# Branch B of a hybrid decoder layer: log-decays in one full-row product, the samples' state products in row quarters, outputs one step later, and a gated residual added out of PSUM

## The chip, the cores and the metric

The kernel runs on 1 core of one Trainium2 chip. The metric is the device time of one execution in microseconds (us), lower is better; a kernel's number is the median of its runs.

## The reference

One inference step of one decoder layer (D = 1024) in float32, for a prompt of 512 tokens and for 8 sample sequences of 8 new tokens each with their own state. The 576 token columns share all weights. The layer is

- `x += 1/2 gate1 * SwiGLU1(mod(rmsnorm(x)))`
- `x += gate2 * W_out(sum_i sigmoid(gate_i(h)) * proj_i(branch_i(h)))` with the branches A (dilated window attention), B (Mamba-2 SSD scan) and C (a gated linear recurrence)
- `x += 1/2 gate3 * SwiGLU2(mod(rmsnorm(x)))`, then a last rmsnorm

The gates come per sequence: one vector for the prompt, one for each of the 8 samples. Branch B matters here. Per head (16 heads of 64 channels, state size 128, 2 groups) and with `acum` the running sum of the log-decays inside a chunk of 128 tokens, the scan computes

```
y_diag[l]   = sum_{s<=l} (C_l . B_s) exp(acum_l - acum_s) xdt[s]
state_out   = sum_s B_s  xdt[s] exp(acum_end - acum_s)
h_next      = exp(acum_end) h + state_out
y[l]        = y_diag[l] + exp(acum_l) C_l . h
```

The prompt is 4 chunks (c = 0 to 3) from a zero state. The samples are 8 chunks of 8 tokens, each from its given `state_ssm`; each writes a new state (1024 x 128).

## The kernel before

**The main work.** `run` goes through a list of units: each is a block of 128 output channels with a weight `raw` of 128 x 1024. ACT casts it to fp32r (`wh`, L278), DVE or, in some units, POOL subtracts to get the remainder `wl` (L280), and TensorE makes for each of 8 k-chunks three fp32r products of 128 x 288 in two halves (L342: H with `wh`, H with `wl`, L with `wh`) into a two-bank PSUM tile `mm`. Six matmuls are one k-chunk, and the main products follow one another on TensorE all along the kernel.

**Lanes.** Between k-chunks `step` advances generators ("lanes") that issue the layer's other work: attention, norms, the recurrence, and `ssd` for branch B. A unit lists its lanes with a number of steps (5 for `ssd`), so the order of every engine is fixed by these numbers at build time; `later` puts a cast or a subtraction one or two turns back. Small products take one of four PSUM banks of the pool `px` in turn; a new tile waits until the bank's last reader is done.

**Branch B, prompt** (`ssd`, L1031). For 20 items (c, hg), c = 0 to 4 and hg = 0 to 3 (four heads each; c = 4 is the 64 sample columns), the work is a pipeline of stages, one item further with each step of the lane: `stage_a` (n), `stage_b` (n-1), `stage_c` (n-2), `stage_d` (n-3).

- `diagonal(c)` (L1083) lays the 16 heads' log-decays out as 16 rows x 4L columns and splits them into a high part `dgH` (ACT) and a remainder `dgL` (DVE).
- `stage_a` broadcasts four heads' decays to 128 partitions: two fp32r matmuls from 16 rows, `dgH` then `dgL`, 512 columns each (256 for c = 4), into `pb` (L1103). So there are 16 pairs of 512 columns and 4 of 256. ACT makes exponents `M` and `Cs` from `pb`.
- `stage_c` multiplies: `M` with the masked C.B on DVE (L1128), `Cs` with C on POOL (L1131).
- `stage_d` makes the outputs `py` on TensorE (L1143, L1146), and DVE adds them into `acc` (L1150).
- `prelude(c+1)` transposes the next chunk in the same steps (`px_tok`, `px_cb`, two `px_xt`, L1047 to L1071). At hg = 0 `state(c-1)` makes the new state: DVE decays it (L1158), two products `pst` (L1162), and DVE adds them in two halves (L1167).

**Branch B, samples** (L1204 to L1258). For each of 8 samples: load the state `st` (`ld`, two ahead), transpose it (`px_st`, 8 transpositions, ACT copies to `sT`), then in `products` 16 small output products `yo` (L1221) and, in two halves q, four products `px_ns` (L1228) of 64 rows, where a mask `bm` leaves one sample's 8 tokens. DVE decays and adds the state (L1231, L1233), and POOL's queue stores it.

**Residual** (`residual`, L700). For each of 56 blocks DVE adds gate x product to `x` (L705, prompt columns). For the 64 sample columns, it multiplies the product in PSUM by the eight gates into a small SBUF tile `rs` (L710), then adds that to `x` (L712).

Of the kernel before, what the change touches and what calls it, by code (L numbers as in the profile page):

```python
# [39 lines left out]
def _consts():  # L40
    c = {}
# [8 lines left out]
    for s in range(64):  # L50
        bmask[s, s // 8] = 1.0
# [4 lines left out]
    for h in range(16):  # L56
        pick[h, h // 4] = pick[h, 4 + h % 4] = 1.0
# [72 lines left out]
class Kern:  # L130
# [245 lines left out]
    def start(self, load, split):  # L376
# [7 lines left out]
        self.gsel, self.qsel = mats[0:16, 337:341], mats[0:16, 341:345]  # L384
# [41 lines left out]
        nc.vector.memset(self.eps, 1e-6)  # L426
        self.G = [self.C([128, 8, 9], f"G{l}") for l in range(3)]
# [271 lines left out]
    def residual(self, j, ps, gidx, hf):  # L699
# [7 lines left out]
        if hf:  # L707
            t = self.s(64, name="rs")
            tv = t.rearrange("p (b t) -> p b t", t=8)
            nc.vector.tensor_tensor(out=tv, in0=ps[:, 1, 224:288].rearrange("p (b t) -> p b t", t=8),  # L710
                                    in1=g[:, 1:9].unsqueeze(2).to_broadcast([128, 8, 8]), op=ALU.mult)
            nc.vector.tensor_tensor(out=x[:, 512:576], in0=x[:, 512:576], in1=t, op=ALU.add)  # L712
# [318 lines left out]
    def ssd(self):  # L1031
# [10 lines left out]
        def prelude(c):  # L1042
# [5 lines left out]
            nc.tensor.transpose(px[0:L, 256:352], self.tok[0:96, cs], self.ident[0:96, 0:96])  # L1048
# [28 lines left out]
        hsel = self.B(512, F32R, "hsel")[0:16, :]  # L1077
        nc.vector.tensor_copy(hsel.rearrange("p (g m) -> p g m", g=4), self.gsel.unsqueeze(2).to_broadcast([16, 4, 128]))
        diag = {}

        def diagonal(c):

            L, cs = (128 if c < 4 else 64), cols(c)  # L1083
            t = self.B(512, name="dg")
            H = self.B(512, F32R, "dgH")
            Lo = self.B(512, F32R, "dgL")
            v = lambda a: a[0:16, 0:4 * L]
            nc.vector.tensor_tensor(out=v(t).rearrange("p (q l) -> p q l", q=4),
                                    in0=self.tok[0:16, cs].unsqueeze(1).to_broadcast([16, 4, L]),
                                    in1=self.qsel.unsqueeze(2).to_broadcast([16, 4, L]), op=ALU.mult)  # L1090
            self.later(1, lambda: nc.scalar.copy(v(H), v(t)))
            self.later(2, lambda: nc.vector.tensor_tensor(out=v(Lo), in0=v(t), in1=v(H).bitcast(F32), op=ALU.subtract))
            diag[c] = (v(H), v(Lo))
# [79 lines left out]
        for n in range(len(items) + 3):  # L1173
            if 0 <= n - 3:
                stage_d(*items[n - 3])
# [1020 lines left out]
```

## Time and profile before

| what | value |
|---|---|
| median of 3 runs | 2119.22 us (2118.07 to 2120.66) |
| the profiled execution | 2117.58 us, its span 2115.6 us |
| mean granted TensorE clock | 0.990 |
| PE (matmul) busy | 2051.7 us, 97% of the span |
| DVE, ACT, POOL busy | 947.6, 834.2, 265.3 us (45%, 39%, 13%) |
| DMA | 304.19 MB, mean 144 GB/s |

"Busy" is the time in which an engine had an instruction in work. PE is busy nearly all the time, so the table says that the kernel is a stream of TensorE work, and not which piece of it can be left out; that is read from the timelines. In a timeline row the number after the engine's instruction (x4) counts instructions run together, and a float32 matmul counts as two. The ends of matmuls are modelled and overlap the next one's start, so the time that a matmul takes from the others is read from starts: this is how the rows of the sections below are to be read.

### The profile page before, as it was taken

What the parts mean: (1) busy time and instruction counts of PE and PEld (TensorE: products, weight loads), DVE (VectorE), ACT (ScalarE), POOL (GpSimd) and SP (SyncE); (2) the same over time, 40 slices, a digit from 0 to 9 for tenths busy, and PEclk for the clock granted to TensorE, in tenths of its full rate; (3) what the DMA queues carried; (4) which work ended last, traced back from release to release, by engine and by line L of the source; (5) the groups of instructions that cost most, each with busy time, mean ns of one, the idle gap of its engine ahead of it and who ended that gap; (6) DMA issues with size and microseconds to landing.
All of it is one profiled execution on the core that took longest, in us unless ns stands there. A gap on an engine that the chain in (4) does not pass through costs nothing.

```text
span 2115.6 us, 40600 instructions
## 1 busy us (share of the span) xinstructions
PE 2051.7 (97%) x17124; PEld 1923.2 (91%) x17124; DVE 947.6 (45%) x1762; ACT 834.2 (39%) x1508; POOL 265.3 (13%) x346
## 2 busy tenths in 40 slices
PE   7999999998999999999999979999999999999997
PEld 6888999998897799999999878888988899999997
DVE  4323323346667546224543574535346723323344
ACT  5222222136656326224342646555424623122132
POOL 2000000015002211000010231101126400000002
PEclk9999999999999999999999999999999999999999
DMA  9756232335541366432233265887878532222222
GB/s 280 255 164 210 78 88 82 92 91 167 180 116 48 97 208 200 126 103 83 71 108 82 62 206 168 275 286 230 270 251 248 160 90 87 84 80 86 83 83 73
DMA packets 381086, 304.19 MB, mean 144 GB/s; under 512 B 16176, under 2 KB 329125, under 8 KB 380904
## 3 DMA queue, kind: packets, MB, share of 16 engines
q1 hardware_dynamic: 370888, 271.15, 43.1%
q0 software_dynamic: 10016, 30.44, 4.2%
q8 instruction: 135, 2.21, 0.5%
q14 instruction: 47, 0.39, 0.1%
HBM read 269.88 MB, written 31.66 MB: 143 GB/s over the span
## 4 chain that ended last, share of the span: by engine, by line
PE 65%; DVE 6%; ACT 2%; DMA 2%; issue 1%; SPq 1%; POOL 0%; POOLq 0%; DVEq 0%; ACTq 0%
PE mm L342 53%; PE kt L1726 2%; PE S L1714 1%; PE O L1819 1%; PE px_ns L1228 1%; PE px_lru L1880 1%; PE po L1498 1%; SPq L170 1%; PE sc L1442 1%; PE px_ld L591 1%; DVE x L712 1%; DVE wl L280 1%; DMA ck<-cache_win_kv 1%; PE pt L1481 1%; DVE M L1128 1%
## 5 line engine op out<-in xcount | busy, mean ns | idle before, releaser
L342 PE MATMUL mm<-H,wh 128*128 128x288 f32 x4112 | 960.3, 306 | 16.0 <-ACT H L694 5.0
L342 PE MATMUL mm<-L,wh 128*128 128x288 f32 x4112 | 918.5, 296 | 1.7 <-DVE L L2064 0.9
L342 PE MATMUL mm<-H,wl 128*128 128x288 f32 x4112 | 917.9, 296 | 0.8 <-POOL wl L280 0.6
L342 PEld LDWEIGHTS mm<-H,wh 128*128 128x128 f32 x4112 | 668.0, 189 | 79.8 <-issue 55.4
L342 PEld LDWEIGHTS mm<-L,wh 128*128 128x128 f32 x4112 | 673.3, 188 | 3.8 <-DVE L L181 1.7
L342 PEld LDWEIGHTS mm<-H,wl 128*128 128x128 f32 x4112 | 672.9, 188 | 2.0 <-POOL wl L280 0.8
L280 DVE TENSOR_TENSOR wl<-raw,wh 128x1024 fp32r<-128x1024 f32 (+1 forms) x241 | 289.9, 1205 | 266.7 <-ACT wh L278 247.0
L278 ACT CAST wh<-raw 128x1024 fp32r<-128x1024 f32 (+2 forms) x289 | 289.6, 1009 | 104.6 <-PE mm L342 95.1
L280 POOL TENSOR_TENSOR wl<-raw,wh 128x1024 fp32r<-128x1024 f32 (+2 forms) x48 | 102.1, 2133 | 720.8 <-ACT wh L278 715.2
L705 DVE SCALAR_TENSOR_TENSOR x<-mm,modT,x 128x288 f32<-128x288 f32 (+1 forms) x112 | 50.9, 480 | 164.6 <-PE mm L342 164.6
L723 ACT ACTIVATE su<-mm 128x576 f32<-128x576 f32 x42 | 27.4, 652 | 238.6 <-PE mm L342 238.6
L180 ACT CAST H<-su 128x576 fp32r<-128x576 f32 x44 | 29.6, 674 | 232.1 <-DVE su L731 225.4
L731 DVE TENSOR_TENSOR su<-su,mm 128x576 f32<-128x576 f32 x42 | 31.7, 755 | 141.9 <-PE mm L342 141.9
L1731 ACT COPY KT<-kt 128x512 f32<-128x512 f32 x78 | 45.6, 588 | 77.6 <-PE kt L1726 67.2
L952 DVE SCALAR_TENSOR_TENSOR acc<-raw,v,acc 128x512 f32<-128x512 f32 x120 | 54.3, 521 | 45.6 <-ACT acc L949 45.5
L1726 PE MATMUL kt<-mats,ck 128*128 128x128 f32 x416 | 64.3, 278 | 10.0 <-DMA ck<-cache_win_kv 8.3
L1726 PEld LDWEIGHTS kt<-mats,ck 128*128 128x128 f32 x416 | 51.5, 143 | 12.3 <-DMA ck<-cache_win_kv 8.5
L1474 ACT ACTIVATE lg<-lg,neg 128x128 f32<-128x128 f32 (+1 forms) x96 | 39.9, 419 | 29.2 <-DVE neg L1465 28.1
L1952 DVE TENSOR_TENSOR sg<-sg,mm 128x576 f32<-128x576 f32 x24 | 18.0, 752 | 68.0 <-PE mm L342 46.5
L181 DVE TENSOR_TENSOR L<-su,H 128x576 fp32r<-128x576 f32 x44 | 33.4, 759 | 32.7 <-ACT H L180 32.7
L639 ACT ACTIVATE sq<-x 128x288 f32<-128x288 f32 x48 | 21.3, 444 | 67.7 <-DVE x L712 35.7
L1729 DVE COPY KT<-kt 128x512 f32<-128x512 f32 x26 | 17.9, 690 | 55.8 <-PE kt L1726 48.3
(388 smaller groups left out, 1742.3 us busy)
## 6 DMA issues: line engine op xcount, KB each, us to landing
raw<-w_in SPq DMA_DIRECT2D x96, 512.0 KB
raw<-w_ff_in SPq DMA_DIRECT2D x88, 512.0 KB
ada<-w_ada SPq DMA_DIRECT2D x72, 512.0 KB
ck<-cache_win_kv SPq DMA_DIRECT2D x52, 512.0 KB
cv<-cache_win_kv SPq DMA_DIRECT2D x52, 512.0 KB
raw<-w_ff_out SPq DMA_DIRECT2D x32, 512.0 KB
raw<-w_ff_out SPq DMA_DIRECT2D x32, 384.0 KB
raw<-w_out SPq DMA_DIRECT2D x16, 512.0 KB
```

Source lines behind the costliest of these rows:

```text
L180: self.later(delay[0], lambda: nc.scalar.copy(H, src))
L181: self.later(delay[1], lambda: nc.vector.tensor_tensor(out=L, in0=src, in1=H.bitcast(F32), op=ALU.subtract), L)
L278: nc.scalar.copy(H, r)
L280: self.later(0 if i < 4 else 2, lambda: e.tensor_tensor(out=L, in0=r, in1=H.bitcast(F32), op=ALU.subtract), L)
L342: nc.tensor.matmul(ps[:M, hf, :HALF], wt[:, k, :], x[:, hf * HALF:(hf + 1) * HALF], start=(k == 0 and p == 0), stop=(k == nk - 1 and p == 2))
L705: nc.vector.scalar_tensor_tensor(out=x[:, c0:c0 + n], in0=ps[:, hf, 0:n], scalar=g[:, 0:1], in1=x[:, c0:c0 + n], op0=ALU.mult, op1=ALU.add)
L723: nc.scalar.activation(t.rearrange("p (a b) -> p a b", a=2), ps[:, :, :HALF], AF.Silu)
L731: nc.vector.tensor_tensor(out=tv, in0=tv, in1=ps[:, :, :HALF], op=ALU.mult)
L952: nc.vector.scalar_tensor_tensor(out=o, in0=i, scalar=w[:, k, j:j + 1], in1=o, op0=ALU.mult, op1=ALU.add)
L1474: nc.scalar.activation(e, e, AF.Exp, bias=neg[:, a:a + 1], accum_out=st[:, a, 1, h:h + 1])
L1726: nc.tensor.transpose(ps[:, j * 128:(j + 1) * 128], t[:, q, j * 128:(j + 1) * 128], self.ident)
L1731: nc.scalar.copy(kt, ps)
```

## The change

1. **Log-decays in one product.** `diagonal` now fills one tile `dgD` of 128 rows: 0 to 31 the high part, 32 to 63 the remainder, 64 to 127 zeros, which POOL copies from a column of zeros. `hsel` has 128 rows that select from both parts, and `stage_a` makes one matmul of 128 rows instead of two of 16. The transposition of `tok` takes 128 rows instead of 96.
2. **Outputs one step later.** `stage_d` works on item n-4 instead of n-3, so the lane has one more step.
3. **Samples in pairs.** Samples b and b+4 go together, in 4 rounds. Their products `px_ns` read 32 rows each (tokens 0 to 31 and 32 to 63) in turn, into two banks. The mask is made once for both. Loads and stores of the states come in pairs.
4. **Residual.** The sample columns' gate product is written back in place in PSUM, and the addition reads it there; the tile `rs` is gone.

```diff
...
     for s in range(64):
-        bmask[s, s // 8] = 1.0
+        bmask[s, s // 8 % 4] = 1.0
     sel = np.zeros((128, 9), np.float32)
...
     for h in range(16):
-        pick[h, h // 4] = pick[h, 4 + h % 4] = 1.0
+        pick[h, h // 4] = pick[32 + h, h // 4] = pick[h, 4 + h % 4] = 1.0
     c["c_mats"] = np.concatenate([ident, tri, blk, bmask, sel, pick], 1)
...
         self.sel = mats[:, 328:337]
-        self.gsel, self.qsel = mats[0:16, 337:341], mats[0:16, 341:345]
+        self.gsel, self.qsel = mats[:, 337:341], mats[0:32, 341:345]
         ct = [self.B(512, name="c") for _ in range(2)]
...
         nc.vector.memset(self.eps, 1e-6)
+        self.zero = self.C([64, 1], "zero")
+        nc.vector.memset(self.zero, 0.0)
         self.G = [self.C([128, 8, 9], f"G{l}") for l in range(3)]
...
         if hf:
-            t = self.s(64, name="rs")
-            tv = t.rearrange("p (b t) -> p b t", t=8)
-            nc.vector.tensor_tensor(out=tv, in0=ps[:, 1, 224:288].rearrange("p (b t) -> p b t", t=8),
-                                    in1=g[:, 1:9].unsqueeze(2).to_broadcast([128, 8, 8]), op=ALU.mult)
-            nc.vector.tensor_tensor(out=x[:, 512:576], in0=x[:, 512:576], in1=t, op=ALU.add)
+            p = ps[:, 1, 224:288]
+            pv = p.rearrange("p (b t) -> p b t", t=8)
+            nc.vector.tensor_tensor(out=pv, in0=pv, in1=g[:, 1:9].unsqueeze(2).to_broadcast([128, 8, 8]), op=ALU.mult)
+            nc.vector.tensor_tensor(out=x[:, 512:576], in0=p, in1=x[:, 512:576], op=ALU.add)
 
...
                 nc.tensor.transpose(px[0:L, g * 128:(g + 1) * 128], xbc[8 + g][:, cs], self.ident)
-            nc.tensor.transpose(px[0:L, 256:352], self.tok[0:96, cs], self.ident[0:96, 0:96])
+            nc.tensor.transpose(px[0:L, 256:384], self.tok[:, cs], self.ident)
             bt = self.B(352, name="bt")
...
 
-        hsel = self.B(512, F32R, "hsel")[0:16, :]
-        nc.vector.tensor_copy(hsel.rearrange("p (g m) -> p g m", g=4), self.gsel.unsqueeze(2).to_broadcast([16, 4, 128]))
+        hsel = self.B(512, F32R, "hsel")
+        nc.vector.tensor_copy(hsel.rearrange("p (g m) -> p g m", g=4), self.gsel.unsqueeze(2).to_broadcast([128, 4, 128]))
         diag = {}
...
 
+
             L, cs = (128 if c < 4 else 64), cols(c)
             t = self.B(512, name="dg")
-            H = self.B(512, F32R, "dgH")
-            Lo = self.B(512, F32R, "dgL")
-            v = lambda a: a[0:16, 0:4 * L]
-            nc.vector.tensor_tensor(out=v(t).rearrange("p (q l) -> p q l", q=4),
-                                    in0=self.tok[0:16, cs].unsqueeze(1).to_broadcast([16, 4, L]),
-                                    in1=self.qsel.unsqueeze(2).to_broadcast([16, 4, L]), op=ALU.mult)
-            self.later(1, lambda: nc.scalar.copy(v(H), v(t)))
-            self.later(2, lambda: nc.vector.tensor_tensor(out=v(Lo), in0=v(t), in1=v(H).bitcast(F32), op=ALU.subtract))
-            diag[c] = (v(H), v(Lo))
+            D = self.B(512, F32R, "dgD")
+            v = lambda a, r: a[r:r + 32, 0:4 * L]
+            nc.vector.tensor_tensor(out=v(t, 0).rearrange("p (q l) -> p q l", q=4),
+                                    in0=self.tok[0:32, cs].unsqueeze(1).to_broadcast([32, 4, L]),
+                                    in1=self.qsel.unsqueeze(2).to_broadcast([32, 4, L]), op=ALU.mult)
+            nc.gpsimd.tensor_copy(D[64:128, 0:4 * L], self.zero.to_broadcast([64, 4 * L]))
+            self.later(1, lambda: nc.scalar.copy(v(D, 0), v(t, 0)))
+            self.later(2, lambda: nc.vector.tensor_tensor(out=v(D, 32), in0=v(t, 0), in1=v(D, 0).bitcast(F32), op=ALU.subtract))
+            diag[c] = D[:, 0:4 * L]
 
...
             pb = self.px("pb")
-            for n, t in enumerate(diag[c]):
-                nc.tensor.matmul(pb[:, 0:4 * L], hsel[:, hg * 128:(hg + 1) * 128], t, start=(n == 0), stop=(n == 1))
+            nc.tensor.matmul(pb[:, 0:4 * L], hsel[:, hg * 128:(hg + 1) * 128], diag[c], start=True, stop=True)
             M = self.B(512, name="M")
...
         nxt = None
-        for n in range(len(items) + 3):
-            if 0 <= n - 3:
-                stage_d(*items[n - 3])
+        for n in range(len(items) + 4):
+            if 0 <= n - 4:
+                stage_d(*items[n - 4])
             if 0 <= n - 1 < len(items):
...
 
-        def products(b, t, sT, bm):
+        def outputs(b, sT):
             for h in range(16):
...
                                  skip_group_check=True)
-            for q in range(2):
-                p = self.px("px_ns")
-                for i in range(4):
-                    j = q * 4 + i
-                    nc.tensor.matmul(p[:, i * 128:(i + 1) * 128], xe[0:64, j * 128:(j + 1) * 128],
-                                     bm[0:64, q * 128:(q + 1) * 128], start=True, stop=True)
-                tv = t[:, q * 4:q * 4 + 4, :]
-                nc.vector.tensor_tensor(out=tv, in0=tv, in1=decv[:, q * 4:q * 4 + 4, b:b + 1].to_broadcast([128, 4, 128]),
-                                        op=ALU.mult)
-                nc.vector.tensor_tensor(out=tv, in0=tv, in1=p.rearrange("p (j n) -> p j n", j=4), op=ALU.add)
-                if q == 0:
-                    yield
-            self.store(view(self.O["s_ssm"][0, b]), t)
+
 
         ld(0)
-        ld(1)
+        ld(4)
         yield
-        for b in range(8):
-            t = sts.pop(b)
-            if b + 2 < 8:
-                ld(b + 2)
-            sT = self.W([1024], F32, "sT")
-            for q in range(2):
-                p = self.px("px_st")
-                for i in range(4):
-                    nc.tensor.transpose(p[:, i * 128:(i + 1) * 128], t[:, q * 4 + i, :], self.ident)
-                nc.scalar.copy(sT[:, q * 512:(q + 1) * 512], p)
+        for b in range(4):
+            if b + 1 < 4:
+                ld(b + 1)
+                ld(b + 5)
+            two = [sts.pop(b), sts.pop(b + 4)]
+            sT = []
+            for t in two:
+                sT.append(self.W([1024], F32, "sT"))
+                for q in range(2):
+                    p = self.px("px_st")
+                    for i in range(4):
+                        nc.tensor.transpose(p[:, i * 128:(i + 1) * 128], t[:, q * 4 + i, :], self.ident)
+                    nc.scalar.copy(sT[-1][:, q * 512:(q + 1) * 512], p)
+                yield
             bm = self.B(256, name="bm")
...
             yield
-            yield from products(b, t, sT, bm)
+            for n in range(2):
+                outputs(b + 4 * n, sT[n])
+            for q in range(2):
+                ps = [self.px("px_ns") for _ in range(2)]
+                for i in range(4):
+                    j = q * 4 + i
+                    for n, p in enumerate(ps):
+                        nc.tensor.matmul(p[:, i * 128:(i + 1) * 128], xe[32 * n:32 * n + 32, j * 128:(j + 1) * 128],
+                                         bm[32 * n:32 * n + 32, q * 128:(q + 1) * 128], start=True, stop=True)
+                for n, p in enumerate(ps):
+                    tv = two[n][:, q * 4:q * 4 + 4, :]
+                    nc.vector.tensor_tensor(out=tv, in0=tv, in1=decv[:, q * 4:q * 4 + 4, b + 4 * n:b + 4 * n + 1].to_broadcast([128, 4, 128]),
+                                            op=ALU.mult)
+                    nc.vector.tensor_tensor(out=tv, in0=tv, in1=p.rearrange("p (j n) -> p j n", j=4), op=ALU.add)
+                yield
+            for n in range(2):
+                self.store(view(self.O["s_ssm"][0, b + 4 * n]), two[n])
             yield
```

Three places show the order of the instructions. The first is DVE and TensorE at the step behind the last `pst` (boundary of chunks 3 and 4). Here is DVE before, from the product `M` of item (3,2) on; `S` is the state, `acc` the branch's output rows, and `M_7196` is the product of item (3,3):

```order
L1128 TENSOR_TENSOR M_7152<-M_7152,cbm_6906 128x512
L280 TENSOR_TENSOR wl_7216<-raw_7010,wh_7215 128x1024
L1158 TENSOR_TENSOR S_7255<-S_7068,decb_6910 128x1024
L1167 TENSOR_TENSOR S_7255<-S_7255,pst_7257 128x512
L1167 TENSOR_TENSOR S_7255<-S_7255,pst_7260 128x512
L1150 SCALAR_TENSOR_TENSOR acc_5808<-acc_5808,dsk,py_7275 128x128
L1150 SCALAR_TENSOR_TENSOR acc_5896<-acc_5896,dsk,py_7275 128x128
L1128 TENSOR_TENSOR M_7196<-M_7196,cbm_6906 128x512
```

and TensorE before, at the second step behind it:

```order
L1103 MATMUL pb_7289<-dgH_7040,hsel_6424 128x256
L1103 MATMUL pb_7289<-dgL_7041,hsel_6424 128x256
L342 MATMUL mm_7218<-H_4791,wh_6815 128x288 x2
L342 MATMUL mm_7218<-H_4791,wl_6816 128x288 x2
L342 MATMUL mm_7218<-L_4792,wh_6815 128x288 x2
L1143 MATMUL py_7304<-M_7196,xd_6908 64x128
```

DVE now, from the same product (`M_7104`):

```order
L1129 TENSOR_TENSOR M_7104<-M_7104,cbm_6864 128x512
L280 TENSOR_TENSOR wl_7167<-raw_6965,wh_7166 128x1024
L1159 TENSOR_TENSOR S_7205<-S_7022,decb_6868 128x1024
L1168 TENSOR_TENSOR S_7205<-S_7205,pst_7207 128x512
L1168 TENSOR_TENSOR S_7205<-S_7205,pst_7210 128x512
L1151 SCALAR_TENSOR_TENSOR acc_5613<-acc_5613,dsk,py_7225 128x128
L1151 SCALAR_TENSOR_TENSOR acc_5696<-acc_5696,dsk,py_7225 128x128
L1129 TENSOR_TENSOR M_7147<-M_7147,cbm_6864 128x512
```

and TensorE now:

```order
L1104 MATMUL pb_7239<-dgD_6995,hsel_6402 128x256
L342 MATMUL mm_7169<-H_4776,wh_6774 128x288 x2
L342 MATMUL mm_7169<-H_4776,wl_6775 128x288 x2
L342 MATMUL mm_7169<-L_4777,wh_6774 128x288 x2
L1144 MATMUL py_7253<-M_7104,xd_6866 64x128
```

DVE's order is the same, but the output `py` that TensorE makes there read the product `M` behind the state's additions before, and now reads the one ahead of them.

The second is TensorE in the first sample's round, from the outputs `yo` on (`sT` a transposed state, `mm` the main products). Before:

```order
L1221 MATMUL yo_7498<-Css_7110,sT_7512 64x8 x16
L1228 MATMUL px_ns_7555<-bm_7525,xe_7109 128x128 x4
L342 MATMUL mm_7472<-H_4791,wh_7215 128x288 x2
L342 MATMUL mm_7472<-H_4791,wl_7216 128x288 x2
L342 MATMUL mm_7472<-L_4792,wh_7215 128x288 x2
L1228 MATMUL px_ns_7568<-bm_7525,xe_7109 128x128 x4
```

Now:

```order
L1222 MATMUL yo_7463<-Css_7064,sT_7484 64x8 x16
L1222 MATMUL yo_7463<-Css_7064,sT_7503 64x8 x16
L1255 MATMUL px_ns_7583<-bm_7528,xe_7063 128x128
L1255 MATMUL px_ns_7584<-bm_7528,xe_7063 128x128
L1255 MATMUL px_ns_7583<-bm_7528,xe_7063 128x128
L1255 MATMUL px_ns_7584<-bm_7528,xe_7063 128x128
L1255 MATMUL px_ns_7583<-bm_7528,xe_7063 128x128
L1255 MATMUL px_ns_7584<-bm_7528,xe_7063 128x128
L1255 MATMUL px_ns_7583<-bm_7528,xe_7063 128x128
L1255 MATMUL px_ns_7584<-bm_7528,xe_7063 128x128
L342 MATMUL mm_7544<-H_4770,wh_7320 128x288 x2
L342 MATMUL mm_7544<-H_4770,wl_7321 128x288 x2
```

Two samples' outputs stand together, and eight products of half the rows alternate between two banks where four stood.

The third is POOL's queue at the boundary of chunks 1 and 2 (`sgd<-z` is a store that waits for ACT). Before:

```order
L173 DMA sgd<-z_6812 128x576
L1131 TENSOR_TENSOR Cs_6763<-Cs_6763,acc_6381 128x512
L1131 TENSOR_TENSOR Cs_6801<-Cs_6801,acc_6381 128x512
L1131 TENSOR_TENSOR Cs_6857<-Cs_6857,acc_6298 128x512
L1131 TENSOR_TENSOR Cs_6919<-Cs_6919,acc_6298 128x512
```

Now:

```order
L173 DMA sgd<-z_6771 128x576
L1132 TENSOR_TENSOR Cs_6727<-Cs_6727,acc_6359 128x512
L1092 CAST dgD_6799<-zero 64x512
L1132 TENSOR_TENSOR Cs_6760<-Cs_6760,acc_6359 128x512
L1132 TENSOR_TENSOR Cs_6815<-Cs_6815,acc_6276 128x512
L1132 TENSOR_TENSOR Cs_6876<-Cs_6876,acc_6276 128x512
```

The zeros of the next chunk's tile (`CAST dgD`) stand between two `Cs` products.

## Rows read from the trace of the kernel before

**Rows 1.** Busy time, sample part: PE, PEld, DVE, ACT, POOL, TensorE clock, DMA share, GB/s
```profile
728.00:800.00 72.00, 72.00 (x746) 67.09 (x745) 31.18 (x55) 19.29 (x30) 11.30 (x15) 1.00 0.68 206
```

**Rows 2.** Timeline of PE, transpositions alone: start us, duration us, instruction
```profile
631.78 0.60 PE L1069 MATMUL px_xt<-mats,acc 128*128 128x128 f32 x4
632.14 0.51 PE L342 MATMUL mm<-H,wh 128*128 128x288 f32 x2
632.49 0.42 PE L342 MATMUL mm<-H,wl 128*128 128x288 f32 x2
632.75 0.43 PE L342 MATMUL mm<-L,wh 128*128 128x288 f32 x2
```

**Rows 3.** Timeline of PE, the same transpositions with a log-decay pair
```profile
638.65 0.60 PE L1069 MATMUL px_xt<-mats,acc 128*128 128x128 f32 x4
639.18 0.50 PE L1103 MATMUL pb<-dgH,hsel 16*128 16x512 f32 x1
639.53 0.39 PE L1103 MATMUL pb<-dgL,hsel 16*128 16x512 f32 x1
639.85 0.53 PE L342 MATMUL mm<-H,wh 128*128 128x288 f32 x2
640.22 0.42 PE L342 MATMUL mm<-H,wl 128*128 128x288 f32 x2
```

**Rows 4.** Timeline of PE, one half of a sample's state products
```profile
736.39 0.42 PE L342 MATMUL mm<-L,wh 128*128 128x288 f32 x2
736.74 1.16 PE L1228 MATMUL px_ns<-bm,xe 64*128 64x128 f32 x8
737.83 0.53 PE L342 MATMUL mm<-H,wh 128*128 128x288 f32 x2
738.20 0.43 PE L342 MATMUL mm<-H,wl 128*128 128x288 f32 x2
```

**Rows 5.** Timeline of PE, attention scores in alternating 64-row halves
```profile
978.08 1.16 PE L1442 MATMUL sc<-k,q 64*128 64x128 f32 x16
979.17 0.53 PE L342 MATMUL mm<-H,wh 128*128 128x288 f32 x2
979.54 0.42 PE L342 MATMUL mm<-H,wl 128*128 128x288 f32 x2
```

**Rows 6.** Waits of PE, 625 to 860 us: total us, times, longest us
```profile
PE pb L1103 <- DVE S L1167: 2.4, 2, 1.3
PE py L1143 <- DVE M L1128: 2.3, 3, 1.7
```

**Rows 7.** Busy time as in rows 1, two short stretches
```profile
710.00:720.00 10.00, 10.00 (x58) 8.55 (x54) 1.73 (x6) 4.39 (x14) 0.78 (x2) 0.51 0.28 77
493.00:507.00 14.00, 8.12 (x54) 7.40 (x55) 12.98 (x27) 10.03 (x18) 9.42 (x7) 1.00 0.72 226
```

**Rows 8.** Timeline of DVE, boundary of chunks 1 and 2
```profile
662.75 2.81 DVE L1128 TENSOR_TENSOR M<-M,cbm 128x512 f32<-128x512 f32 x1
665.48 1.76 DVE L1088 TENSOR_TENSOR dg<-tk,mats 16x512 f32<-16x512 f32 x1
...
669.62 1.29 DVE L1167 TENSOR_TENSOR S<-S,pst 128x512 f32<-128x512 f32 x2
```

**Rows 9.** Timeline of POOL, the same stretch
```profile
662.48 4.22 POOL L1131 TENSOR_TENSOR Cs<-Cs,acc 128x512 f32<-128x512 f32 x3
```

**Rows 10.** DVE by line: busy us, mean ns, idle before
```profile
L712 DVE TENSOR_TENSOR x<-x,rs 128x64 f32<-128x64 f32 x56 | 31.0, 554 | 1.9
...
L710 DVE TENSOR_TENSOR rs<-mm,modT 128x64 f32<-128x64 f32 x56 | 12.0, 214 | 0.0
```

**Rows 11.** Timeline of SP's DMA queue, sample part
```profile
746.18 9.77 SPq L170 DMA_DIRECT2D st<-state_ssm  x2
758.72 0.37 SPq L170 DMA_DIRECT2D raw<-w_in  x1
```

**Rows 12.** Timeline of ACT, the cast of the weights loaded in rows 11
```profile
783.47 1.05 ACT L278 CAST wh<-raw 128x1024 fp32r<-128x1024 f32 x1
```

## Prediction

> **What bounds the kernel now.** The windows by stage come first: where the samples' states are made TensorE is busy 72.00 of 72.00 us at the full clock [rows 1]; so in branch B a TensorE instruction less is time less, and work on another engine costs only where TensorE waits for it. The timelines of TensorE are read next, by starts: one pair of main matmuls starts 0.26 us after another [rows 2], and what other work adds is the longer distance around it. Then the waits: between 625 and 860 us TensorE stands still 2.4 us in two places for the state's addition and 2.3 us for the product M [rows 6]. Last the clock: from 710 to 720 us, right behind the longest of these waits (1.7 us), TensorE ran at a granted clock of 0.51, the lower of its two levels (1.2 against 2.4 GHz) [rows 7]. The profiled execution took 2117.58 us, 1.64 less than the median; all terms are differences within it, so I put them on the median of 2119.2.
>
> **Log-decays in one product.** Four transpositions alone hold up the main products so that the second pair starts 0.71 us behind the first transposition (631.78 to 632.49) [rows 2]; with a log-decay pair behind them it is 1.57 us (638.65 to 640.22) [rows 3]. The pair costs 0.86 us there; the two matmuls by themselves 0.67 (639.18 to 639.85). The one that stays has 512 columns and all 128 rows like the main ones: 0.13 us for 288 columns makes 0.24 for 512, an estimate. So each pair saves between 0.67 - 0.24 = 0.43 and 0.86 - 0.24 = 0.62 us. I take 0.55, nearer to the upper end, since the slow first main pair behind the 16-row matmuls (0.37 us) goes too. 16 x 0.55 = 8.8, and 4 pairs of half the columns at half of it 1.1: **-9.9 us** (-7.8 to -11.2). The 128-row transposition of `tok` replaces one of 96 rows: nothing.
>
> **The zeros.** POOL makes five copies of 64 x 512 (one of 64 x 256). No row has one. A product of two operands over 128 x 512 takes 1.41 us there (4.22 for three) [rows 9]; a copy reads one, so I take half, 0.7 us, bounds 0 and 1.4. It matters where it stands between two `Cs` products at a chunk's boundary: beside those three products DVE's M took 2.81 us and the next product 1.76 [rows 8]; the subtraction of the weights, S and its additions follow them on DVE, and the first half of S (released some 0.65 us after 669.62, half of the row's 1.29) is what `pb` waited for, in a bank that `pst` held. Two such waits are 2.4 us [rows 6]. Now TensorE comes there some 0.55 earlier (one pair less since the chain's start) and the chain some 0.7 later: 2 x 1.25 = **+2.5 us** (+1.1 with the zeros hidden, +4.0 with the full product's price).
>
> **Outputs one step later.** Every `py` reads an M made a step earlier, so the three waits of 2.3 us for M [rows 6] go. At the boundary of chunks 3 and 4 the new `py` needs M of the item before, which DVE makes ahead of the state's additions, but its PSUM bank is that of the first `pst`. DVE frees that ahead of the state's second half, two output additions and M, so about the whole 1.7 us wait lies behind it; but with TensorE early by two half pairs some 0.4 us of a wait remain: **-1.9 us** (-2.3 to 0). If the 1.7 us wait sets off the low clock behind it, the clock's loss goes too: 10 us at 0.51 instead of 1.00 are **-4.9 us** (0 to -4.9) [rows 7]. I take it whole, since the fall begins where that wait ends. The lane ends one step later; the norm behind it comes one k-chunk, three pairs of 0.26, closer to the projection that reads it: **+0.8 us** (0 to +0.8).
>
> **Samples in pairs.** Half a sample's products hold the second main pair behind them to 1.81 us after the pair ahead (736.39 to 738.20) where two distances of 0.26 would be 0.52: 1.29 us [rows 4], 16 times. After the change there are 8 groups, each with twice the matmuls, from two sets of rows in turn. The nearest row is the attention scores: 16 matmul rows of 64-row halves in turn into two banks take 1.46 us to the second pair [rows 5], just what 8 in one half take (736.74 to 738.20, 1.46) [rows 4]. So the second half was free there, and I take the same for quarters: 8 groups less, 8 x 1.29 = **-10.3 us** (-1.6 if they don't overlap, below).
>
> The Trainium skill's page "TensorE: Matmul & The Clock Gate", Part 3 (Measured speedup vs the span model), says that matmuls in different row tiles run at once but that four tiles of 32 rows gave 3.07 times and not four; shared out, two would give about 1.54 and not 2, and by that estimate the term would be some 2.8 us smaller. In rows 4 and 5 two halves gave 2.0; no run here shows quarters.
>
> Bank waits: `yo` keeps one of four banks, so the second q's two tiles need one that DVE must free first. One addition of a 128 x 512 product takes 0.65 us (two in 1.29) [rows 8], and the order leaves 6 or 12 main matmuls (0.8 or 1.6 us) between: **+0.5 us** over the four rounds (0 to +2). Half of the masks go (DVE, hidden: TensorE doesn't wait for DVE in rows 1). Loads in pairs hold two more weight buffers; see the last rival.
>
> **Residual.** The 56 additions take 31.0 us, 554 ns each, against 214 ns for the multiplication of the same size out of PSUM [rows 10]. About 19 us of it (31.0 - 56 x 0.214) is waiting inside the instruction, at places where POOL is busy with its share of the weights' remainders: between 493 and 507 us POOL works 9.42 of 14 us and TensorE stands for 5.9 [rows 7]. With a PSUM operand the addition may pass there; but the square sums and the norm's products behind it read SBUF alone and meet POOL's work instead. So **0 us**: bounds -5.9 (all idle of that stretch) and +3 (half of it the other way, if the products behind are blocked worse; the PSUM tile is also held for one addition longer).
>
> The Trainium skill's "VectorE: DVE Perf Modes" (errata section, cycle table) gives a PSUM source 62 cycles at 0.96 GHz more than an SBUF source, a rule against this edit; by it 56 additions would take 3.6 us more of DVE. The trace disagrees at this size: out of PSUM 64 columns take 214 ns [rows 10].
>
> **Sum.** -9.9 + 2.5 - 1.9 - 4.9 + 0.8 - 10.3 + 0.5 + 0 = -23.2: 2094.4 for an execution like the profiled one, **2096 us** on the median.
>
> **Rivals.**
> *The clock falls elsewhere.* The waits for the state's addition grow from 1.3 to some 2.6 us, longer than the 1.7 that stood ahead of the fall. Against it: between 493 and 507 us TensorE stood for 5.9 of 14 us, and the clock stayed 1.00 [rows 7], so a wait alone doesn't decide. One fall more costs 4.9: 2101; two, or one with the old fall kept, 2106.
> *Quarters don't overlap.* Each group then takes twice the 1.09 us of its products (736.74 to 737.83): 8 x 1.09 = 8.7 given back, 2104.7. For it: no row has 32 rows; against it: rows 5.
> *The residual pays.* The blocked additions pass POOL and the stretch at 493 us closes up: -5.9, 2090.
> *Weights come late; slower than before.* SP's queue is in order, and a state's load that waits for a buffer holds the weights' loads behind it: two state loads took 9.77 us to be issued, and the weights behind them went out at 758.72 [rows 11]; ACT cast them at 783.47 [rows 12]. So the lead is 24.7 us. Each round now puts two loads there before the pair's stores are done. It decides from the point where a pair's block is longer than that lead: then three rounds wait by about another 9.8 us, +29 and with the sum +6: 2125. Against it: a blocked queue took under half of the lead.
> *The step does nothing.* The waits for M turn into waits for the bank of equal length and the low clock stays: +1.9 + 4.9, 2102.8.
>
> **How the numbers follow.** Forecast 0.48; the clock elsewhere 0.24; no overlap 0.10; the step does nothing 0.07; residual 0.06; weights late 0.05. The range from 2088 to 2109 takes in all but the last and the case that two of them meet, and the bounds of the terms that can go together: log-decays at their best, the bank waits at their worst. Under 0.2% (4.2 us) can't be told from no change here. Faster by more: all cases but the last and some sums of two, 0.92; within 0.2%: 0.04; slower: 0.04.
>
> **What would show it.** Right: one `pb` matmul per item, the second main pair about 1.0 us behind the transpositions instead of 1.57; each `px_ns` group of 16 at 1.46 us to the second pair; no wait of `py` for M, `pb` waits of some 2.5 us; a granted clock near 1.00 from 710 to 720 us. Wrong: `px_ns` groups of 2.5 us, a low clock in a new place, waits of the main products for weights past 740 us, or TensorE's idle around 493 us changed by more than 2 us.

## The result, and the profile after

The changed kernel takes **2097.7 us** (median of 4 runs, 2093.7 to 2101.4) against 2118.8 before: a ratio of 0.9899, 95% interval 0.9879 to 0.9919. That is 21 us less, where 23.2 were forecast and 2096 us. Its profiled execution took 2096.72 us.

The starts of the same main matmul in both profiled executions show where the difference arises (times are those of the kernel before). The changed kernel is 1.3 us behind at 604 us, just ahead of branch B, 15.4 ahead at 728, where the samples' states begin, and 25.6 at 834; at the lane's end it loses 1.3, at 1600 it is 26.6 ahead, and between 1600 and 1680 it loses 4.5. So branch B gave more than the whole difference, and another place took some of it back.

The changed kernel's page, span and busy time:

```profile
span 2094.9 us, 40560 instructions
...
PE 2030.4 (97%) x17104; PEld 1911.1 (91%) x17104; DVE 952.2 (45%) x1759; ACT 832.8 (40%) x1508; POOL 271.6 (13%) x351
```

TensorE is as full as before. It is busy 21.3 us less (2051.7 to 2030.4), which is the whole gain of the execution; its idle time sums to about the same.

**Log-decays.** The timeline of TensorE at the transpositions that rows 3 show, now with one product of 128 rows:

```profile
638.75 0.60 PE L1070 MATMUL px_xt<-mats,acc 128*128 128x128 f32 x4
639.11 0.48 PE L1104 MATMUL pb<-dgD,hsel 128*128 128x512 f32 x1
639.42 0.43 PE L342 MATMUL mm<-H,wh 128*128 128x288 f32 x2
639.69 0.43 PE L342 MATMUL mm<-H,wl 128*128 128x288 f32 x2
```

The second main pair comes 0.94 us behind the first transposition (638.75 to 639.69) instead of 1.57 [rows 3]: 0.63 saved. The pairs behind the product are 0.27 apart, not 0.37.

**State products.** One half of a round, two samples at once (a float32 matmul counts as two, so x16 are eight products):

```profile
727.18 0.42 PE L342 MATMUL mm<-L,wh 128*128 128x288 f32 x2
727.53 1.16 PE L1255 MATMUL px_ns<-bm,xe 32*128 32x128 f32 x16
728.62 0.53 PE L342 MATMUL mm<-H,wh 128*128 128x288 f32 x2
729.00 0.43 PE L342 MATMUL mm<-H,wl 128*128 128x288 f32 x2
```

Sixteen matmul instructions of two quarters hold the main products up as long as eight of one half did: 1.82 us from pair to pair (727.18 to 729.00), 1.81 before [rows 4].

**Waits and clock.** TensorE's waits from 600 to 860 us (total us, times, longest us), where rows 6 show those before:

```profile
PE pb L1104 <- DVE cbm L1058: 1.8, 2, 1.1
PE mm L342 <- DVE L L181: 1.2, 1, 1.2
PE py L1144 <- DVE S L1168: 0.8, 1, 0.8
PE px_xt L1070 <- DVE acc L1151: 0.2, 1, 0.2
```

The waits for M are gone and so are those of `pb` for S; in their place `pb` waits for the masked product `cbm`, `py` for the first `pst` bank (0.8; 0.4 forecast), and the main products 1.2 us for the remainder L at the lane's end (0.2 before; 0.8 more forecast). Three windows (PE, PEld, DVE, ACT, POOL, clock, DMA share, GB/s):

```profile
695.00:715.00 20.00, 19.17 (x182) 17.00 (x183) 12.43 (x26) 8.49 (x24) 4.08 (x6) 1.00 0.55 155
490.00:500.00 10.00, 7.72 (x47) 7.51 (x46) 9.86 (x18) 7.99 (x16) 7.76 (x7) 0.83 0.74 240
1630.00:1640.00 10.00, 7.65 (x45) 6.25 (x46) 9.79 (x18) 6.41 (x12) 6.09 (x3) 0.83 0.31 107
```

The place where the clock was 0.51 [rows 7] now runs at 1.00; new are two stretches at 0.83, at the ends of the two feed-forward parts, where the residual's additions stand close. A low clock in a new place was one of the prediction's signs of being wrong, and it is answered below: the residual's part explains the second stretch, not the first.

**The chain at a chunk's boundary.** VectorE, to be read beside rows 8, and POOL, beside rows 9:

```profile
658.02 1.79 DVE L1129 TENSOR_TENSOR M<-M,cbm 128x512 f32<-128x512 f32 x1
659.73 1.08 DVE L1089 TENSOR_TENSOR dg<-tk,mats 32x512 f32<-32x512 f32 x1
...
663.18 1.29 DVE L1168 TENSOR_TENSOR S<-S,pst 128x512 f32<-128x512 f32 x2
...
666.58 1.42 DVE L1129 TENSOR_TENSOR M<-M,cbm 128x512 f32<-128x512 f32 x1
667.92 0.41 DVE L1058 TENSOR_TENSOR cbm<-px_cb,mats 128x256 f32<-128x256 f32 x1
```

```profile
657.94 1.30 POOL L1132 TENSOR_TENSOR Cs<-Cs,acc 128x512 f32<-128x512 f32 x1
659.31 0.96 POOL L1092 CAST dgD<-zero 64x512 fp32r<-64x512 f32 x1
660.35 5.12 POOL L1132 TENSOR_TENSOR Cs<-Cs,acc 128x512 f32<-128x512 f32 x2
```

The zeros take 0.96 us here (0.7 forecast), but they didn't lengthen the chain. The next product of POOL no longer starts right behind the first: M got through in 1.79 us instead of 2.81, and now it is POOL's two products that take 5.12. The first half of S was there in time, and what came late was the next step's M (1.42) and `cbm` behind it.

### The profile page after: what moved, and what is told of

Same layout as the page of the kernel before. It is cut to its first block, busy times and chain, and to the rows that moved or that the text cites. A ratio compares the mean times of both kernels' runs of the same rounds, so it can differ in the third digit from the quotient of the medians.

```text
span 2094.9 us, 40560 instructions
## 1 busy us (share of the span) xinstructions
PE 2030.4 (97%) x17104; PEld 1911.1 (91%) x17104; DVE 952.2 (45%) x1759; ACT 832.8 (40%) x1508; POOL 271.6 (13%) x351
## 4 chain that ended last, share of the span: by engine, by line
PE 65%; DVE 6%; DMA 2%; ACT 2%; issue 1%; SPq 1%; POOL 0%; POOLq 0%; DVEq 0%; ACTq 0%
PE mm L342 53%; PE kt L1735 2%; PE S L1723 1%; PE O L1828 1%; SPq L170 1%; PE px_ld L593 1%; PE px_lru L1889 1%; PE sc L1451 1%; PE po L1507 1%; DVE sq L646 1%; DMA cv<-cache_win_kv 1%; DVE wl L280 1%; DMA ck<-cache_win_kv 1%; PE pt L1490 1%; DVE L L699 0%
## 5 line engine op out<-in xcount | busy, mean ns | idle before, releaser
L641 ACT ACTIVATE sq<-x 128x288 f32<-128x288 f32 x48 | 21.3, 443 | 64.2 <-DVE x L713 32.1
```

## The experiments

Each was timed beside the kernel before on the same chip; there were three sessions on three chips (runs 1 to 4, 5 to 8, 9 to 12), and that kernel's medians were 2118.8, 2119.9 and 2119.7 us. The ratio is to that kernel, with its 95% interval; across sessions the ratios are the safer comparison.

| run | what it has | median us | ratio |
|---|---|---|---|
| 1 | before, with the residual alone | 2123.1 | 1.0016 (1.0007 to 1.0025) |
| 2 | changed, with the residual of before | 2093.3 | 0.9878 (0.9865 to 0.9890) |
| 3 | before, with outputs one step later alone | 2114.4 | 0.9975 (0.9965 to 0.9985) |
| 4 | changed, with outputs at n-3 | 2113.2 | 0.9972 (0.9962 to 0.9981) |
| 5 | before, with the log-decay product alone | 2112.3 | 0.9972 (0.9960 to 0.9983) |
| 6 | before, with the samples in pairs alone | 2111.5 | 0.9965 (0.9950 to 0.9979) |
| 7 | run 2's kernel, quarters in sequence | 2105.0 | 0.9932 (0.9919 to 0.9946) |
| 8 | run 2's kernel, log-decays from 64 rows, no zeros | 2100.9 | 0.9910 (0.9897 to 0.9923) |
| 9 | before, with log-decays and outputs later | 2102.9 | 0.9919 (0.9907 to 0.9932) |
| 10 | run 2's kernel again | 2092.8 | 0.9872 (0.9857 to 0.9887) |
| 11 | run 10's kernel, output products split | 2094.1 | 0.9878 (0.9864 to 0.9892) |
| 12 | run 10's kernel, output products apart | 2094.7 | 0.9878 (0.9865 to 0.9892) |

### Runs 1 and 2: the residual

Run 1 is the kernel before with the change's part 4, run 2 the changed kernel without it:

```diff
-            p = ps[:, 1, 224:288]
-            pv = p.rearrange("p (b t) -> p b t", t=8)
-            nc.vector.tensor_tensor(out=pv, in0=pv, in1=g[:, 1:9].unsqueeze(2).to_broadcast([128, 8, 8]), op=ALU.mult)
-            nc.vector.tensor_tensor(out=x[:, 512:576], in0=p, in1=x[:, 512:576], op=ALU.add)
+            t = self.s(64, name="rs")
...
+            nc.vector.tensor_tensor(out=x[:, 512:576], in0=x[:, 512:576], in1=t, op=ALU.add)
```

> The kernel before with the residual of the change alone. Theory: the edit costs time. The addition is no longer blocked, but the products behind it on VectorE are, in front of the next unit's PSUM reader: in the changed kernel TensorE waited 4.7 us (two times 2.4) near 490 us and 2.3 us near 1637 us for the residual's addition, and the clock was 0.83 in two stretches of 10 us. Against the waits of the kernel before (5.9 us and 1.4 us) and with two clock falls this is slower by 2 to 5 us. Rival A: the edit saves what it was made for, 2 to 6 us faster. Rival B: it does nothing, within 1.5 us, and the loss near 1660 us came from the shifted timing of the rest.

> The changed kernel with the residual of before. Theory: 2 to 5 us faster than the changed kernel, some 2093 to 2095 us, with waits near 490 and 1640 us for the casts H again and a clock of 1.00 there. Rival: the same as the changed kernel, 2097 to 2098 us.

Measured: alone, the edit makes the kernel 3.4 us slower by the ratio (0.16%, interval 0.07% to 0.25%; 4.3 by the medians); without it the change is 4.4 us faster (run 2) and 4.9 (run 10) by the medians, though the intervals of the ratios touch that of the changed kernel. The profiles settle it: by the starts of the main matmuls between 1600 and 1680 us, the three kernels that have the edit (changed, runs 1 and 4) lose 4.5, 3.1 and 3.0 us against the kernel before, and the other ten lose nothing (0.2 at most). The theory's sign and size hold. Its account of the waits holds in one place only. Near 490 us run 2 waits as the kernel before did, 5.9 us, and its clock fell there too (0.86 from 500 to 510 us), so that stretch gave the edit nothing to answer for. At the end of the second feed-forward part, 1620 to 1670 us, TensorE stood 4.5 us in the changed kernel, 3.0 in run 1, and 1.4 without the edit (before and run 2), at a clock of 0.97 against 1.00. So 1.6 of run 1's 3.1 us are the longer wait; the rest goes with the clock. How the wait comes about is in three timelines of the changed kernel, VectorE, POOL and TensorE:

```profile
1633.34 2.63 DVE L699 TENSOR_TENSOR L<-t,H 128x288 fp32r<-128x288 f32 x1
1635.90 0.44 DVE L707 SCALAR_TENSOR_TENSOR x<-mm,modT,x 128x224 f32<-128x224 f32 x1
1636.37 0.23 DVE L712 TENSOR_TENSOR mm<-mm,modT 128x64 f32<-128x64 f32 x1
1636.63 0.22 DVE L713 TENSOR_TENSOR x<-mm,x 128x64 f32<-128x64 f32 x1
```

```profile
1633.15 2.50 POOL L280 TENSOR_TENSOR wl<-raw,wh 128x1024 fp32r<-128x1024 f32 x1 [1.16 <-ACT wh L278]
```

```profile
1637.01 0.58 PE L342 MATMUL mm<-H,wh 128*128 128x288 f32 x1 [2.35 <-DVE x L713]
```

The addition (L713) takes 0.22 us and is never blocked. The norm's subtraction ahead of it (L699) takes 2.63, beside POOL's 2.50, and TensorE waits 2.35 us for the PSUM tile that the addition releases. Before, the blocked instruction was the addition itself, and it read SBUF: the PSUM tile had been released by the multiplication ahead of it. The block moved from behind the release to ahead of it. By line it is nearly the same time: the two residual lines went from 43.0 us [rows 10] to 25.6,

```profile
L713 DVE TENSOR_TENSOR x<-mm,x 128x64 f32<-128x64 f32 x56 | 12.6, 224 | 1.9
...
L712 DVE TENSOR_TENSOR mm<-mm,modT 128x64 f32<-128x64 f32 x56 | 13.0, 232 | 1.9
```

while the square sums went from 29.1 us to 38.0,

```profile
L644 DVE TENSOR_TENSOR sq<-sq,sq 128x288 f32<-128x288 f32 x40 | 29.1, 727 | 1.3 <-ACT sq L639 0.7
...
L646 DVE TENSOR_TENSOR sq<-sq,sq 128x288 f32<-128x288 f32 x40 | 38.0, 951 | 0.6
```

and the norm's two lines from 17.3 to 19.5 and from 14.5 to 18.9: together 15.5 of the 17.4 us that the residual's lines lost. Run 1 has the same figures (38.2, 19.5, 18.9) without the rest of the change.

### Runs 3, 4, 5 and 9: log-decays and outputs

Run 4 puts `stage_d` back to n-3 in the changed kernel; run 3 has n-4 alone, run 5 the log-decay product alone, run 9 both.

```diff
-        for n in range(len(items) + 4):
-            if 0 <= n - 4:
-                stage_d(*items[n - 4])
+        for n in range(len(items) + 3):
+            if 0 <= n - 3:
+                stage_d(*items[n - 3])
```

> The kernel before with the outputs one step later and nothing else. Theory: the 1.7 us wait of py for M goes, with it the low clock from 710 to 720 us: 2.3 + 4.9 us less, 0.8 us more at the lane's end, so 6 us faster (2112 to 2113), with the clock at 1.00 there. Rival: the wait goes but the clock falls as before, set off by something else: 1 to 2 us faster.

> The changed kernel with the outputs at n-3 again. Theory: TensorE waits for M at the boundaries of the chunks, 2 to 4 us in all, the longest over 1.7 us, and the clock falls behind it: 6 to 8 us slower than the changed kernel, 2104 to 2106. Rival: the wait comes back but no clock fall: 2 to 3 us slower, about 2100.

> The kernel before with the log-decays in one product and nothing else; outputs at n-3. Theory: the 20 pairs still save some 10 to 11 us of TensorE time, but TensorE then reaches the outputs earlier than VectorE has M, as in the changed kernel with n-3 (8.8 us of waits for M against 4.7 us of waits in all before), and a clock fall stays: 3 to 7 us faster than before, 2112 to 2116. Rival: the saving comes through in full, 10 us faster, 2109, waits for M as before.

> The kernel before with the log-decays in one product and the outputs one step later, nothing else. Theory: the two parts need each other. Alone they gave 7.5 and 4.4 us; together the waits for M that ate a third of the first (8.7 us) go too, so 15 to 17 us faster than before: 2102 to 2104. Rival: they add up, 12 us: 2107.

Run 3: 5 us faster by the ratio (3 to 7), the forecast 6. Its waits from 600 to 860 us show no M left, and from 700 to 720 us the clock is 1.00:

```profile
PE pb L1103 <- DVE S L1167: 2.3, 2, 1.3
PE mm L342 <- DVE L L181: 1.2, 1, 1.2
```

```profile
700.00:720.00 20.00, 20.00 (x176) 16.38 (x172) 15.31 (x27) 8.54 (x28) 6.52 (x8) 1.00 0.48 138
```

Its profile has a fall in another place (0.85 from 690 to 700 us), so the gain is not the whole clock loss. That fall stands right behind a wait of `pb` for S (1.28 us), and runs 1 and 8 have one behind the same wait (1.36 and 1.52 us; clock 0.66 from 691 to 696 and 0.60 from 686 to 690 us); the kernel before had that wait (1.34) and no fall behind it. The fall at the lane's end is steadier: all five profiles with the outputs at n-3 have it (before, runs 1, 4, 5 and 6: clocks of 0.51 to 0.66 within 707 to 720 us), and none of the nine at n-4. Run 4 was a miss of size: 15.5 us slower than the changed kernel, twice what was expected (its profiled execution, the fastest of nine, lost 11.6). Its waits for M are 8.8 us:

```profile
PE py L1144 <- DVE M L1129: 8.8, 4, 2.8
```

Run 5 has nearly the same, and gives 6 us (4 to 8) instead of 10; its clock fell three times, each time at one of these waits (0.66 from 669 to 674 and from 686 to 691, 0.57 from 707 to 711 us):

```profile
PE py L1145 <- DVE M L1130: 8.7, 4, 2.8
```

So TensorE, freed of the pairs, runs into VectorE's M: a good third of the log-decays' saving is paid back unless the outputs come later. Together (run 9) the two give 17 us (14 to 20), where alone they give 6 and 5. The rest of run 4's loss goes with the clock: it fell at the last wait for M (0.66 from 711 to 716 us), and in a place without waits, behind two of the four rounds of samples (below).

### Runs 6 and 7: pairs and quarters

```diff
-                for i in range(4):
-                    j = q * 4 + i
-                    for n, p in enumerate(ps):
+                for n, p in enumerate(ps):
+                    for i in range(4):
+                        j = q * 4 + i
```

> The kernel before with the samples in pairs and row quarters alone. Theory: 8 groups of 1.29 us less, since nothing in that stage waits for another engine: 10 us faster, 2108 to 2109. Rival: part of it is lost to bank waits or late states: 5 to 8 us faster.

> The changed kernel with the residual of before, and the eight products of a round's half in sequence: four of one quarter, then four of the other, instead of in turn. Theory: the gain is overlap of neighbours in different quarters, so in sequence each group takes twice the 1.09 us: 8 x 1.09 = 8.7 us slower than the same kernel in turn (2093.3), 2102. Rival: the order doesn't matter, 2093 to 2094.

Run 6: 7 us by the ratio (4 to 11), 8 by the medians; the 10 expected lie inside, and its profile has one fall of the clock in the stage (0.83 from 740 to 750 us). Run 7 is 11.7 us slower than run 2 (11.4 by the ratios); the rival falls. But the theory's own price was too high. In sequence (timeline of TensorE):

```profile
723.70 2.04 PE L1223 MATMUL yo<-Css,sT 128*64 128x8 f32 x64
725.67 1.71 PE L1256 MATMUL px_ns<-bm,xe 32*128 32x128 f32 x16
727.31 0.54 PE L342 MATMUL mm<-H,wh 128*128 128x288 f32 x2
727.68 0.43 PE L342 MATMUL mm<-H,wl 128*128 128x288 f32 x2
727.95 0.59 PE L342 MATMUL mm<-L,wh 128*128 128x288 f32 x2
728.47 3.09 PE L1256 MATMUL px_ns<-bm,xe 32*128 32x128 f32 x16
```

These sixteen instructions take 1.64 us to the next main pair (725.67 to 727.31), not 2.18: the quarters overlap in part in sequence and wholly in turn (1.09). For the eight groups that is 8 x 0.55 = 4.4 us. The rest of the 11.7 goes with the clock, here ahead of and behind those rows (columns as in rows 1):

```profile
723.00:727.00 4.00, 4.00 (x85) 3.81 (x84) 0.14 (x1) 1.58 (x2) 0.54 (x1) 1.00 0.63 202
729.00:733.00 4.00, 4.00 (x22) 3.78 (x21) 3.79 (x6) 0.00 (x0) 0.90 (x1) 0.50 0.02 5
```

TensorE was busy throughout, with 32 products of 8 columns (x64 in the trace), the quarters, and three main pairs; then the granted clock fell to 0.50 until about 735 us. That happened in each of this profile's four rounds. In run 4 it happened behind the same work in turn, in two rounds of four (742 to 746 at 1.00, 748 to 752 at 0.50), in run 6 and run 8 in one, and in the changed kernel and run 2 in none, though their rounds hold the same work. Run 4:

```profile
742.00:746.00 4.00, 4.00 (x87) 3.69 (x87) 0.26 (x1) 1.47 (x2) 0.57 (x1) 1.00 0.97 282
748.00:752.00 4.00, 4.00 (x23) 3.78 (x22) 3.79 (x6) 0.00 (x0) 0.90 (x1) 0.50 0.06 16
```

### Run 8: 64 rows, no zeros

```diff
-            nc.gpsimd.tensor_copy(D[64:128, 0:4 * L], self.zero.to_broadcast([64, 4 * L]))
...
-            diag[c] = D[:, 0:4 * L]
+            diag[c] = D[0:64, 0:4 * L]
...
-            nc.tensor.matmul(pb[:, 0:4 * L], hsel[:, hg * 128:(hg + 1) * 128], diag[c], start=True, stop=True)
+            nc.tensor.matmul(pb[:, 0:4 * L], hsel[0:64, hg * 128:(hg + 1) * 128], diag[c], start=True, stop=True)
```

> The changed kernel with the residual of before, and the log-decay product from 64 rows only (high part and remainder), so that POOL copies no zeros. Theory: what made the pair dear was also the change to few rows and back, seen as a first main pair 0.37 us apart behind it instead of 0.27 and as a later start; with 64 rows this comes back: 0.15 to 0.3 us for each of 20, 3 to 6 us slower, 2096 to 2099, less what the zeros cost (0 to 1 us). Rival: full rows bring nothing, the halving was all: the same or 1 us faster, 2092 to 2093.

It is 7.6 us slower than run 2 (6.8 by the ratios), more than expected. The run changes the rows and the copy together; the rows of the trace tell them apart. One product from 64 rows:

```profile
638.80 0.60 PE L1071 MATMUL px_xt<-mats,acc 128*128 128x128 f32 x4
639.33 0.50 PE L1104 MATMUL pb<-dgD,hsel 64*128 64x512 f32 x1
639.76 0.53 PE L342 MATMUL mm<-H,wh 128*128 128x288 f32 x2
640.13 0.43 PE L342 MATMUL mm<-H,wl 128*128 128x288 f32 x2
```

1.33 us to the second main pair (638.80 to 640.13), against 0.94 from 128 rows and 1.57 for the pair of 16 [rows 3]. So of the 0.63 us only 0.24 came from one product less, and 0.39 from staying on full rows: the product starts 0.53 us behind the first transposition instead of 0.36, the main pair 0.43 behind it instead of 0.31, and the next 0.37 instead of 0.27. The other items of 512 columns without a wait beside them lose 0.38 to 0.40 too, save one (0.30), and those of 256 columns 0.20, so 16 x 0.39 + 4 x 0.20 = 7.0 us. That is about what the run lost, but its profile also has two falls of the clock that run 2's doesn't (0.60 from 686 to 690, 0.50 from 762 to 768 us), so part of the loss may be theirs. And without the zeros the boundary is as before, three products of POOL in a row and M beside them:

```profile
660.06 4.23 POOL L1132 TENSOR_TENSOR Cs<-Cs,acc 128x512 f32<-128x512 f32 x3
```

```profile
660.33 2.81 DVE L1129 TENSOR_TENSOR M<-M,cbm 128x512 f32<-128x512 f32 x1
```

`pb` waits 2.8 us for S again, and with `py` (0.2) that is 3.0 us of waits against 2.8 in the changed kernel. So the zeros, a cost in the forecast, cost nothing that the waits show. The block didn't vanish with them: in the changed kernel the next M takes 1.42 us, without them 0.69, as before.

### Runs 10 to 12: the clock in the samples' stage

```diff
             bm = self.B(256, name="bm")
...
+            outputs(b, sT[0])
             yield
-            for n in range(2):
-                outputs(b + 4 * n, sT[n])
+            outputs(b + 4, sT[1])
```

That is run 11; run 12 puts the second sample's outputs into the store's step instead.

> The changed kernel with the residual of before, the same as in the earlier run, as a neighbour for the next two: 2093 to 2094.

> The changed kernel with the residual of before, and the two samples' output products in two steps: the first in the mask's step, the second ahead of the products as before. Theory: in other runs of paired samples the clock fell for some 5 to 8 us right behind the 3 us of output products and state products that stand together; with 1 us of them taken away no fall is left in that stage, at the price of one more change of tile per round (4 x 0.2 us): 2092 to 2094, never above 2097. Rival: the falls there have nothing to do with it, and it is 1 us slower than its neighbour.

> The same with the second sample's output products behind the state products, in the store's step, so that no two such groups stand together. Theory: as the split, two more changes of tile per round (8 x 0.2 us): 2092 to 2095. Rival: the outputs stand right ahead of the next states' transpositions and hold up the additions: 2 us or more slower.

Neither helps: 2094.1 and 2094.7 beside 2092.8, with intervals that overlap. None of the three has a fall in that stage in its profile, so the theory on the falls wasn't tried by them; that the small products set them off is what runs 4 and 7 suggest, and stays open. The fastest kernel is the change without its residual, run 2's and 10's, at 2093 us; runs 11 and 12 can't be told from it.

## Why the prediction was right

The forecast held in direction and size, and in mechanism for the three large terms (log-decays, state products, clock at the lane's end). Two small steps failed, and they cancel: the zeros came out 3.1 us better than forecast, the residual 3.4 worse. That the total lies within about 2 us is in part luck.

| term | forecast us | in the traces |
|---|---|---|
| log-decays | -9.9 | 16 x 0.63 + 4 x 0.30 = -11.3, the upper bound |
| waits of `pb`, with the zeros | +2.5 | 2.4 to 1.8: -0.6 |
| waits of `py` and `px_xt` | -1.9 | 2.3 to 1.0: -1.3 |
| clock at 710 us | -4.9 | 0.51 to 1.00: -4.9 |
| lane's end | +0.8 | waits for L, 0.2 to 1.2: +1.0 |
| state products | -10.3 | 8 groups less, 1.29 each: -10.3 |
| bank waits | +0.5 | none listed: 0 |
| residual | 0 | +3.4 by run 1 |

Their sum is -24.0; the two profiled executions differ by 20.9, the medians by 21.1. By the starts of the main matmuls, the samples gave 10.2 (-10.3 in the table) and the lane's end took 1.3 (+1.0), but the prompt's part, up to 728 us, gave 16.7 where its four terms add up to 18.1, and the residual's place took 4.5 in this execution, not 3.4. The rest nets to almost nothing: 1.3 lost ahead of branch B, 2.4 won between 860 and 1600 us and 1.0 lost behind 1680, where the clock falls at times in either kernel. What the prompt's part lacks isn't pinned down. The parts timed apart agree with the whole: by the ratios runs 9 and 6 gave 17 and 7 us, and run 2, which has both without the residual, 26.

- **Log-decays.** Right, at the upper bound, and for a reason that the forecast only brushed: the change of rows was the larger part (0.39 of 0.63 us by run 8, if a 64-row product costs what a 16-row one does). The condition was missing: alone the saving doesn't come through whole (run 5).
- **The zeros.** The step "the chain some 0.7 later" failed. The price of the copy was right (0.62 to 0.96), but the forecast took who is blocked as given; the copy between the products changed that (M 1.79 instead of 2.81 us), and in run 8, without it, the old order comes back.
- **Outputs later.** Right, the low clock too: run 3 has neither wait nor fall there, nor has any other kernel at n-4.
- **State products.** Right to the hundredth for quarters in turn. By the estimate from the Trainium skill's page "TensorE: Matmul & The Clock Gate", Part 3 (Measured speedup vs the span model), two quarters would have given 1.54; here they gave 2.0 in turn (16 in the 1.09 us of 8) and 1.33 in sequence (1.64).
- **Residual.** The forecast of 0 failed, and at +3.4 the measured cost lies just past its upper bound of +3. The step named the right blocking, but took a block in another instruction of the same engine for a block of the same cost. What counts is whether it stands ahead of the release of the PSUM tile. The rule against the edit in the Trainium skill's page "VectorE: DVE Perf Modes" (errata section, cycle table) isn't the cause: the addition out of PSUM takes 224 ns, as the unblocked ones from SBUF nearly all do in 226 (their median).
- **The rivals.** The clock's falls elsewhere were real. Behind the wait for the state's addition, where I put them, they came in runs 1, 3 and 8, and in the changed kernel, where that wait is gone, not; other falls came behind the samples' rounds (runs 4, 6, 7 and 8) and at the end of the second feed-forward part (changed, runs 1 and 4). The weights never came late: no wait for them in the stage.

## What to carry to other kernels

When two parts of a change touch the same chain, time each alone and both together: here one part's saving was waiting time for the other part's engine, and together they gave half as much again (17 us) as the two apart (6 and 5). A product that keeps to the rows of its neighbours can be worth more than the halved work, and small products from different rows should be issued in turn. Before making an instruction immune to a block by another engine, look where the block goes: here it cost nothing behind the release of a buffer, and ahead of it the bottleneck waited.

## What the runs showed of the hardware that was not expected

- A 64-row product of 512 columns between 128-row ones costs 0.39 us more than the same product padded with zero rows to 128 (1.33 against 0.94 us to the second main pair, run 8).
- Four products of one quarter and then four of the other overlap in part: 1.64 us against 1.09 in turn (run 7).
- VectorE and POOL, working on SBUF at once, hold one another up, and a short POOL instruction in between shifts who waits: M (0.68 us elsewhere) 2.81 and three POOL products 4.22 us became M 1.79 and two POOL products 5.12. Without that instruction M takes 2.81 again (run 8).
- The granted clock fell to its lower level in stretches where TensorE was busy all the time, right behind 3.1 us (run 4, two rounds of four) and 3.6 us (run 7, every round) of small products. The same 3.1 us stood in each round of the changed kernel without a fall, so they don't decide alone.
